# Both halves of the values as one stationary operand, and two places that follow

## The chip, the cores and the metric

The kernel runs on one core of one Trainium2 chip. The metric is the device time of one execution in microseconds, lower is better.

## The reference

Two transformer layers over one sequence of 512 tokens and 1024 features, all in float32. What the change touches is shown here: the values' product of the first layer's attention, the gates beta and the inverse of the second layer's delta rule.

```python
# layer 1, attention of 16 heads of 64, in query blocks of 128 (scores use softplus and a reverse cumsum)
    a = jnp.exp(log_a).astype(v.dtype)
    outs.append(jnp.einsum('bhts,bshd->bthd', a, v[:, :end]))
# layer 2, chunks of 64 tokens, 8 heads
beta = jax.nn.sigmoid(beta_logit)                       # beta_logit, a_dt: 16 columns of x @ w_in
g = -jnp.exp(a_log) * jax.nn.softplus(a_dt + dt_bias)
lower = jnp.where(strict, jnp.einsum('bhncd,bhnmd->bhncm', k_beta, k) * decay, 0.0)
t_inv = lax.linalg.triangular_solve(lower, eye, left_side=True, lower=True, unit_diagonal=True)
```

Around them stand the usual parts: norms, projections, a gated feed-forward part in layer 1, a second mixer (retention) and a squared-ReLU feed-forward part in layer 2.

## The kernel before

Tokens come in NT = 4 tiles of 128 and features in KD = 8 tiles of 128. Nearly every product keeps float32's precision by two rounded numbers for each operand: the upper part h (the value rounded to the fast type F32R) and the lower part l (what is left). `split_w` does this for weights (ACT makes h, DVE makes l), `evac_pair` for results in PSUM. A product then takes three passes (`mm3`): h by h, h by l and l by h; the l by l pass is left out. Small products of plain float32 operands (the delta rule) are single calls that the trace shows as two records each.

The attention of layer 1 (`attention`) is written as a loop over 48 banks, three for each head: the bank holds the scores of some key blocks b against the queries, as `BANKS` says (blocks 3 and 2 with 256 columns each, block 1 with 384, block 0 with 512). For each bank `z_bank` makes the scores, ACT and DVE make the softplus, `sums_bank` adds the cumulative sums by matmuls and makes the weights a, again as h and l, and `av_bank` multiplies them by the values into one PSUM bank of the head ("pso"). `z_bank` runs LAG = 3 banks ahead of `sums_bank`, and `av_bank` one behind. When a head's third bank is through, its result is split into h and l (ACT, then DVE) into the head's half of a pair of slots, which the output projection reads.

Two heads lie side by side in a result of 128 partitions, so a stationary tile of values holds 64 columns of each of two heads (vH or vL), and only one half of the 128 rows of the result is read.

Between the banks `run` lets other work for TensorE go on, the fill: the generator `others` gives the projections of queries and keys of the pairs 1 to 7 (`qk`), those of the values of heads 8 to 15 (`values`), and, at the end, the part of the output projection that is already possible (`out_part`). Each bank may issue BESIDE = 2300 ns of fill, counted in the kernel's own estimate of TensorE's time. When the loop comes to the scores of a pair whose queries are not yet there (`ready_q`), it takes fill without ration until they are. DVE also sums the conditioning's products here (`mod_sums`, L500), two for each of 24 steps.

The order on each engine's queue is set by the tile framework's scheduler from the order in the program, the dependences and its cost estimates. SP's queue issues the loads of weights.

In layer 2 `first_proj` projects the 16 columns of beta and a_dt together with the first heads' queries and keys in two halves of 256 tokens (`halved`), and `gates_and_decays` makes beta and the decays from them. `delta_inverse` builds the inverse of a unit triangular matrix of 128 x 128 in each of 4 chunk pairs of a head, from inverses of 32 x 32 that DVE has solved: it merges twice, and holds the result and its transpose side by side (X, Y), with each merge a few products of 128 x 128, four at a time (`prods`). Two of these generators run turn by turn with the projections and with the scans (`delta_scan`), at distances given by their `yield` values in ns.

Of the kernel before, what the change touches and what calls it, by code (L numbers as in the profile page):

```python
# [10 lines left out]
F32R = mybir.dt.float32r  # L11
# [6 lines left out]
P = 128  # L18
# [52 lines left out]
class Net:  # L71
# [83 lines left out]
    def halved(self, units, xT, first=None):  # L155

        for t0 in (0, 256):
            t = slice(t0, t0 + 256)  # L160
            for i, (acc, h, l) in enumerate(units):
                nk = h.shape[1]
                for k in range(nk):
                    xh, xl = xT[k]
                    self.mm3(acc[:, t], h[:, k, :], l[:, k, :], xh[:, t], xl[:, t],
                             k == 0 and t0 == 0, k == nk - 1, chk=True)
# [451 lines left out]
    def attention(self):  # L618
# [6 lines left out]
        def ev_v(g0):  # L625
            def ev(tt, acc):
                for g in range(g0, g0 + acc.shape[-1] // 256):
                    if tt == 0:
                        v[g] = [self.pair(), self.pair()]
                    t = v[g][tt // 2]  # L630
                    c = slice(tt % 2 * 256, tt % 2 * 256 + 256)
                    self.evac_pair(t[:, 0, c], t[:, 1, c], acc[:, (g - g0) * 256:(g - g0 + 1) * 256])
            return ev
# [57 lines left out]

        def values(g):
            r = self.raw(wqkv, 0, KD, 2 * D + g * 256, 256)
            hl = {}
            for c in (0, 4):
                h, l = self.split_w(r[:, c:c + 4, :], [P, 4, 256])
                for i in range(4):
                    hl[c + i] = (h[:, i, :], l[:, i, :])
            yield
            for tt in range(NT):  # L700
                if tt % 2 == 0:
                    bank = self.ps("g")
                acc = bank[:, tt % 2 * 256:tt % 2 * 256 + 256]
                t = slice(tt * P, (tt + 1) * P)
                for k in range(KD):
                    self.mm3(acc, hT[k][0][:, t], hT[k][1][:, t], *hl[k], k == 0 and tt % 2 == 0, k == KD - 1, chk=True)
                    if k % 4 == 3 and k < KD - 1:
                        yield
                ev_v(g)(tt, acc)
                yield  # L710
# [145 lines left out]
    def av_bank(self, n):  # L856
# [8 lines left out]
        for b, t0, c0, w in self.BANKS[bi]:  # L865
            c = b % 2 * 256 + pr % 2 * P
            vH, vL = self.v[pr // 2][b // 2][:, 0, c:c + P], self.v[pr // 2][b // 2][:, 1, c:c + P]
# [76 lines left out]
    def gates_and_decays(self, acc, heads):  # L944
# [3 lines left out]
        sm = self.t2()  # L948
        nc.vector.tensor_copy(sm[:16, :], acc[:16, :])
        dtb = self.bcast_row(a["dt_bias_2"][0], A_H, "dtb")  # L950
# [4 lines left out]
        for n in range(NT):  # L955
            nc.tensor.transpose(pt[:, n * 16:(n + 1) * 16], sm[:16, n * P:(n + 1) * P], self.ident[:16, :16])
        pv = pt[:, :64].rearrange("p (n c) -> p n c", c=16)

# [84 lines left out]
    def first_proj(self, heads):  # L1043

        nc, w = self.nc, self.a["w_in_2"][0]
        r = self.t2([P, KD, 16])
        nc.sync.dma_start(r, w[:, O_BE:O_BE + 16].rearrange("(k p) c -> p k c", p=P))
        hl = self.t2([P, 2, KD, 16], F32R)
        h, l = hl[:, 0], hl[:, 1]
        self.evac_pair(h, l, r)  # L1050
# [150 lines left out]
    def delta_inverse(self, heads):  # L1201
# [3 lines left out]
        for h in heads:  # L1205
# [484 lines left out]
```

## Time and profile before

| | |
|---|---|
| median of three runs | 2096.71 us (2095.53 to 2097.28) |
| the profiled execution | 2098.39 us, of which its span 2096.6 us |
| granted TensorE clock, mean over the span | 0.997 |
| TensorE (PE) busy | 2056.1 us, 98% of the span |
| VectorE (DVE), ScalarE (ACT), GpSimd (POOL) busy | 54%, 40%, 6% |
| the attention's heads | from about 80 to 298 us |
| gates and first projection of layer 2 | about 703 to 745 us |
| inverses and scans | 887 to 980 us and 1126 to 1230 us |

In the profile a row names line, engine, operation, the tiles written and read (psa, psg and pso are banks of PSUM; "pso<-s,s" from 85 to 298 us is the product with the values), the shape, the count, and then busy time and the mean of one in ns. The columns of matmuls of 512 take 0.39 us each but start every 0.23 us, since they overlap; so a matmul's price is its spacing, not its duration. L135 is the line of `mm`, through which most matmuls go; L269 and L270 are the two halves of `evac_pair`.

### The profile page before, as it was taken

The page shows a single profiled execution, that of the slowest core. Times are in us where ns is not written, and L with a number is a line of the kernel's source. Part 1 is how long each engine was busy: PE and PEld are TensorE (multiplying, and loading weights), DVE is VectorE, ACT ScalarE, POOL GpSimd, SP SyncE. Part 2 cuts the span into 40 slices and gives each one's busy share as a digit, 9 for nine tenths or more (in the row PEclk, how much of TensorE's full clock was granted, in tenths as well). Part 3 has the DMA queues.
Part 4 walks back from the last instruction along what each step waited for, and adds up shares of the span by engine and source line. Part 5 has one row for each costly group of instructions (what it writes and reads, how often), then busy time and mean ns, then how long its engine had stood idle before and what let it go on. Part 6 is the DMA issues. An engine that isn't in the chain of part 4 may idle for free.

```text
span 2096.6 us, 25166 instructions
## 1 busy us (share of the span) xinstructions
PE 2056.1 (98%) x10019; PEld 1724.0 (82%) x10019; DVE 1132.4 (54%) x1835; ACT 838.1 (40%) x1348; POOL 115.8 (6%) x171
## 2 busy tenths in 40 slices
PE   6999999999999999999999999999999999999998
PEld 5788878888888888887888788888888889888886
DVE  6689878333322565866667545344444475423433
ACT  3787764223212364344533432333232344323421
POOL 2000000000000113000320000000000000000000
PEclk9999999999999999999999999999999999999999
DMA  8545545323233344321342343222222553323322
GB/s 266 166 123 151 160 125 177 101 96 115 90 131 101 102 128 133 102 66 41 129 136 73 101 146 121 96 81 86 81 86 81 183 178 121 101 87 125 100 91 81
DMA packets 169687, 244.00 MB, mean 116 GB/s; under 512 B 14097, under 2 KB 112491, under 8 KB 169569
## 3 DMA queue, kind: packets, MB, share of 16 engines
q1 hardware_dynamic: 166092, 234.76, 34.1%
q0 software_dynamic: 3232, 7.34, 1.5%
q8 instruction: 79, 1.29, 0.3%
q14 instruction: 40, 0.32, 0.0%
q10 hardware_dynamic: 244, 0.29, 0.0%
HBM read 218.69 MB, written 19.42 MB: 114 GB/s over the span
## 4 chain that ended last, share of the span: by engine, by line
PE 91%; DVE 4%; DMA 2%; ACT 1%; issue 1%; POOL 1%; POOLq 0%; DVEq 0%; ACTq 0%; SPq 0%
PE psg L135 42%; PE psa L135 37%; PE pso L135 10%; PE psa L139 1%; DMA raw<-sb_w_qkv 1%; DVE wl L126 1%; DVE s L270 1%; DMA s<-ada_w 1%; DMA cv<-ada_w 0%; PE pso L322 0%; DVE s L1370 0%; PE pso L1513 0%; DMA s<-x 0%; PE pso L575 0%; POOL sm L1365 0%
## 5 line engine op out<-in xcount | busy, mean ns | idle before, releaser
L135 PE MATMUL psg<-s,wh 128*128 128x512 f32 x2368 | 744.6, 395 | 1.9 <-DVE s L270 1.7
L126 DVE TENSOR_TENSOR wl<-raw,wh 128x1024 fp32r<-128x1024 f32 x306 | 373.7, 1222 | 461.3 <-ACT wh L122 262.0
L135 PEld LDWEIGHTS psg<-s,wh 128*128 128x128 f32 x2368 | 440.0, 188 | 89.7 <-issue 2.1
L135 PE MATMUL psa<-wh,s 128*128 128x512 f32 x1536 | 479.5, 391 | 0.0
L135 PE MATMUL psg<-s,wl 128*128 128x512 f32 x1184 | 462.4, 391 | 0.0
L122 ACT CAST wh<-raw 128x1024 fp32r<-128x1024 f32 x202 | 212.2, 1053 | 416.5 <-PE psg L135 157.0
L135 PEld LDWEIGHTS psa<-wh,s 128*128 128x128 f32 x1536 | 289.5, 189 | 60.2 <-ACT s L272 0.3
L135 PE MATMUL psa<-wl,s 128*128 128x512 f32 x768 | 299.5, 390 | 0.3 <-DVE wl L126 0.3
L135 PEld LDWEIGHTS psg<-s,wl 128*128 128x128 f32 x1184 | 222.3, 188 | 46.4
L135 PEld LDWEIGHTS psa<-wl,s 128*128 128x128 f32 x768 | 144.8, 188 | 30.4 <-DVE wl L126 0.6
L125 ACT CAST wh<-raw 128x1024 fp32r<-128x1024 f32 x104 | 109.0, 1050 | 138.2 <-PE psg L135 109.0
L135 PE MATMUL psa<-s,s 128*128 128x512 f32 (+3 forms) x712 | 161.1, 359 | 0.0
L135 PEld LDWEIGHTS psa<-s,s 128*128 128x128 f32 x712 | 123.3, 189 | 20.5 <-DVE s L1318 0.9
L135 PE MATMUL pso<-s,wh 128*128 128x512 f32 x448 | 137.9, 389 | 0.0
L135 PE MATMUL psg<-wh,s 128*128 128x512 f32 (+1 forms) x416 | 132.0, 379 | 0.0
L135 PEld LDWEIGHTS pso<-s,wh 128*128 128x128 f32 x448 | 84.1, 188 | 17.5
L135 PE MATMUL pso<-s,wl 128*128 128x512 f32 x224 | 87.1, 389 | 0.0
L135 PEld LDWEIGHTS psg<-wh,s 128*128 128x128 f32 x416 | 75.1, 189 | 11.5 <-DVE s L270 0.4
L269 ACT CAST s<-t 128x512 fp32r<-128x512 f32 (+1 forms) x94 | 54.5, 594 | 59.5 <-DVE t L1604 40.7
L135 PE MATMUL psa<-s,wh 128*128 128x256 f32 x384 | 72.9, 291 | 2.3 <-DVE s L270 1.5
L135 PE MATMUL psg<-wl,s 128*128 128x512 f32 (+1 forms) x208 | 74.9, 360 | 0.0
L270 DVE TENSOR_TENSOR s<-t,s 128x512 fp32r<-128x512 f32 (+1 forms) x94 | 59.7, 654 | 20.1 <-ACT s L269 19.9
(250 smaller groups left out, 2144.9 us busy)
## 6 DMA issues: line engine op xcount, KB each, us to landing
raw<-w_in SPq DMA_DIRECT2D x56, 1024.0 KB, 5.2
raw<-ffn_w_in SPq DMA_DIRECT2D x22, 1024.0 KB, 5.1
cv<-ada_w SPq DMA_DIRECT2D x64, 256.0 KB, 2.8
raw<-w_up SPq DMA_DIRECT2D x16, 1024.0 KB, 5.3
raw<-w_down SPq DMA_DIRECT2D x16, 1024.0 KB, 5.0
raw<-sb_w_qkv SPq DMA_DIRECT2D x10, 1024.0 KB, 7.7
raw<-ffn_w_out SPq DMA_DIRECT2D x10, 1024.0 KB, 6.3
s<-ada_w SPq DMA_DIRECT2D x32, 256.0 KB, 6.6
```

What stands on the lines that cost most here:

```text
L122: nc.scalar.copy(h, src)
L125: nc.scalar.copy(h, src)
L126: nc.vector.tensor_sub(l, src, h.bitcast(F32))
L135: self.last_mm = self.nc.tensor.matmul(acc, lhsT, rhs, **kw)
L139: self.last_mm = self.nc.tensor.transpose(out, x, ident)
L269: nc.scalar.copy(dst_h, src)
L270: nc.vector.tensor_sub(dst_l, src, dst_h.bitcast(F32))
```

## The change

Values: the tiles now hold, for each head, its 64 columns of h beside its 64 columns of l. That tile is stationary, and two passes (the weights' h and l) give h's result in one half of the partitions and l's in the other, for one head. The two halves are added at the end of the head: ACT copies one half to a temporary tile in the head's own half, DVE adds the other half from PSUM, and the sum is split as before. So a head's last step is ACT, DVE, ACT, DVE where it was ACT, DVE. The l by l pass comes with it.

The values of heads 8 to 15 are projected in one go, 512 columns wide, after pair 3's queries, and no longer in two goes of 256 columns after pairs 3 and 5.

Gates: h and l of the 16 columns stand side by side as 32 stationary columns, in two passes; their rows are added after the transpose to tokens (one copy and one addition on DVE more).

Inverse: the transposed result Y1 of the first merge was a product of its own (four matmuls) and is now a transpose of X1 by TensorE, with a copy instead of an addition on DVE. It is made one step later, beside the next product.

```diff
# halved
+                    if l is None:
+                        for x in (xh, xl):
+                            self.mm(acc[:, t], h[:, k, :], x[:, t], start=k == 0 and t0 == 0 and x is xh,
+                                    stop=k == nk - 1 and x is xl, skip_group_check=True)
# attention, ev_v
-                    t = v[g][tt // 2]
-                    c = slice(tt % 2 * 256, tt % 2 * 256 + 256)
-                    self.evac_pair(t[:, 0, c], t[:, 1, c], acc[:, (g - g0) * 256:(g - g0 + 1) * 256])
+                    t = v[g][tt // 2][:, tt % 2, :].rearrange("p (h i d) -> p h i d", h=4, i=2)
+                    x = acc[:, (g - g0) * 256:(g - g0 + 1) * 256].rearrange("p (h d) -> p h d", h=4)
+                    self.evac_pair(t[:, :, 0, :], t[:, :, 1, :], x)
# attention, values and others
-        def values(g):
-            r = self.raw(wqkv, 0, KD, 2 * D + g * 256, 256)
+        def values():
+            for k0 in (0, 4):
+                r = self.raw(wqkv, k0, 4, 2 * D + S, S)
...
-                    self.mm3(acc, hT[k][0][:, t], hT[k][1][:, t], *hl[k], k == 0 and tt % 2 == 0, k == KD - 1, chk=True)
-                    if k % 4 == 3 and k < KD - 1:
+                    self.mm3(acc, hT[k][0][:, t], hT[k][1][:, t], *hl[k], k == 0, k == KD - 1)
+                    if k % 2 == 1 and k < KD - 1:
...
-                if pr in (3, 5):
-                    yield from values((pr + 1) // 2)
+                if pr == 3:
+                    yield from values()
# av_bank
-            mm(out[:, t], vH, ab[:, 0, cc], start=(b == 3), stop=False, skip_group_check=True)
-            mm(out[:, t], vH, ab[:, 1, cc], start=False, stop=False, skip_group_check=True)
-            mm(out[:, t], vL, ab[:, 0, cc], start=False, stop=(b == 0), skip_group_check=True)
+            v = self.v[pr // 2][b // 2][:, b % 2, h % 4 * P:h % 4 * P + P]
+            mm(out[:, t], v, ab[:, 0, cc], start=(b == 3), stop=False, skip_group_check=True)
+            mm(out[:, t], v, ab[:, 1, cc], start=False, stop=(b == 0), skip_group_check=True)
...
-        r = slice(e * 64, e * 64 + 64)
-        self.evac_pair(o[r, 0, :], o[r, 1, :], out[r, :])
+        r, r2 = (slice(i * 64, i * 64 + 64) for i in (e, 1 - e))
+        u = self.t2()
+        self.nc.scalar.copy(u[r, :], out[r2, :])
+        self.nc.vector.tensor_add(u[r, :], u[r, :], out[r, :])
+        self.evac_pair(o[r, 0, :], o[r, 1, :], u[r, :])
# gates_and_decays, first_proj
+        pv = self.const("pv", [P, NT, 16])
+        p2 = pt[:, :128].rearrange("p (n i c) -> p n i c", i=2, c=16)
+        nc.vector.tensor_copy(pv, p2[:, :, 0, :])
+        nc.vector.tensor_add(pv, pv, p2[:, :, 1, :])
...
-        self.qk_proj(0, [(acc[:16, :], h, l)], lambda: self.beside(self.gates_and_decays(acc, heads)))
+        self.qk_proj(0, [(acc[:32, :], hl.rearrange("p k i c -> p k (i c)"), None)], lambda: self.beside(self.gates_and_decays(acc, heads)))
# delta_inverse
-            nc.vector.tensor_add(Y1, Y0, prods(Pm, Y0))
...
-            yield 1200
+            pt = self.ps("a")
+            for n in range(NT):
+                cs = slice(n * P, (n + 1) * P)
+                self.tr(pt[:, cs], X1[:, cs], self.ident)
+            nc.vector.tensor_copy(Y1, pt)
+            yield 1500
```

How it moves instructions is seen at three places. A row gives the line, the operation, the tile written, the tiles read, and the shape; "x3" is three such rows in a run.

First TensorE at the end of the attention's steady fill. "psg" is the output projection's first part, "pso" the product with the values, "psa ... tri" the cumulative sums, "psa<-s,s" the scores. Before, the last steady fill stands ahead of head 13's third bank (bank 41 of 0 to 47):

```order
L135 MATMUL psg_2766<-wl_2758,s_118_2472 128x512
L135 MATMUL psg_2766<-wh_2757,s_118_2472 128x512
L135 MATMUL psa_2801<-s_47_522,tri 128x256 x6
L135 MATMUL pso_2842<-s_133_2878,s_104_2035 128x512 x3
L135 MATMUL psa_2928<-s_129_2724,s_124_2606 128x256 x2
```

After, it stands ahead of head 12's third bank (bank 38):

```order
L135 MATMUL psg_2559<-wl_2551,s_121_2421 128x512
L135 MATMUL psg_2559<-wh_2550,s_121_2421 128x512
L135 MATMUL psa_2586<-s_48_523,tri 128x256 x6
L135 MATMUL pso_2630<-s_129_2661,s_81_1311 128x512 x2
L135 MATMUL psa_2716<-s_125_2514,s_120_2393 128x256 x2
```

Behind both stand six more matmuls of the fill, between later banks; the loop's last banks without steady fill are the six from 42 in the one and the nine from 39 in the other.

Second DVE at the end of a head (head 0), the split of "pso" and what stands around it, before:

```order
L825 TENSOR_TENSOR cr_826<-t_820,cr_825 128x512
L854 TENSOR_TENSOR s_50_525<-t_846,s_50_525 128x384
L270 TENSOR_TENSOR s_61_835<-psg_749,s_61_835 64x512
L270 TENSOR_TENSOR s_62_866<-pso_773,s_62_866 64x512
L815 SCALAR_TENSOR_TENSOR t_877<-psa_869,t_877 128x384
```

After (L830, L859, L275 and L820 are the same lines, L888 is the new addition):

```order
L830 TENSOR_TENSOR cr_823<-t_817,cr_822 128x512
L859 TENSOR_TENSOR s_50_525<-t_843,s_50_525 128x384
L275 TENSOR_TENSOR s_61_832<-psg_749,s_61_832 64x512
L888 TENSOR_TENSOR t_863<-t_863,pso_773 64x512
L820 SCALAR_TENSOR_TENSOR t_876<-psa_868,t_876 128x384
L858 CAST s_63_897<-t_895 128x384
L505 SCALAR_TENSOR_TENSOR s_67_938<-cv_1126,csilu,s_67_938 128x512
L275 TENSOR_TENSOR s_62_862<-t_863,s_62_862 64x512
```

The bank of PSUM is now read by the addition at the place of the old split, and the split follows three rows later.

Third TensorE in the second pair of inverses. Before, each head's first merge takes the product of Y0 and Pm (t_7689 is the first head's Pm, t_7702 the other's) and then that of Pm and Y0:

```order
L135 MATMUL psa_7703<-s_251_7640,s_252_7647 128x128 x4
L135 MATMUL psa_7711<-t_7689,s_249_7608 128x128 x4
L135 MATMUL psa_7717<-s_249_7608,t_7689 128x128 x4
L135 MATMUL psa_7723<-s_238_7170,s_242_7433 128x256
L135 MATMUL psa_7728<-t_7702,s_251_7640 128x128 x4
L135 MATMUL psa_7734<-s_251_7640,t_7702 128x128 x4
L135 MATMUL psa_7740<-s_238_7170,s_225_6453 128x256
L135 MATMUL psa_7744<-t_7709,s_250_7615 128x128 x4
```

After, the second of them is gone and a transpose of X1 (t_7584) stands behind the product that follows:

```order
L135 MATMUL psa_7578<-s_251_7499,s_252_7506 128x128 x4
L135 MATMUL psa_7586<-t_7564,s_249_7483 128x128 x4
L135 MATMUL psa_7592<-s_238_7045,s_242_7308 128x256
L135 MATMUL psa_7597<-t_7577,s_251_7499 128x128 x4
L135 MATMUL psg_7633<-wh_7615,s_204_5556 128x512
L135 MATMUL psg_7633<-wl_7616,s_204_5556 128x512
L135 MATMUL psg_7633<-wh_7615,s_208_5560 128x512
L135 MATMUL psa_7637<-s_238_7045,s_225_6328 128x256
L135 MATMUL psa_7641<-t_7584,s_250_7490 128x128 x4
L139 MATMUL psa_7647<-cst,t_7584 128x128 x4
```

The products that follow have moved up, and three matmuls of a projection stand between the two steps.

More of the change, by code (lines that the diff above doesn't have):

```diff
@@ L164, in halved @@
                     xh, xl = xT[k]
-                    self.mm3(acc[:, t], h[:, k, :], l[:, k, :], xh[:, t], xl[:, t],
-                             k == 0 and t0 == 0, k == nk - 1, chk=True)
+                    if l is None:
+                        for x in (xh, xl):
+                            self.mm(acc[:, t], h[:, k, :], x[:, t], start=k == 0 and t0 == 0 and x is xh,
+                                    stop=k == nk - 1 and x is xl, skip_group_check=True)
+                    else:
+                        self.mm3(acc[:, t], h[:, k, :], l[:, k, :], xh[:, t], xl[:, t],
+                                 k == 0 and t0 == 0, k == nk - 1, chk=True)
                     self.poll()
@@ L690, in qk @@
             yield
-        def values(g):
-            r = self.raw(wqkv, 0, KD, 2 * D + g * 256, 256)
+        def values():
             hl = {}
[L695 to L699, printed above, removed]
+            for k0 in (0, 4):
+                r = self.raw(wqkv, k0, 4, 2 * D + S, S)
+                for c in (0, 2):
+                    h, l = self.split_w(r[:, c:c + 2, :], [P, 2, S])
+                    for i in range(2):
+                        hl[k0 + c + i] = (h[:, i, :], l[:, i, :])
+                    yield
             for tt in range(NT):
-                if tt % 2 == 0:
-                    bank = self.ps("g")
-                acc = bank[:, tt % 2 * 256:tt % 2 * 256 + 256]
+                acc = self.ps("g")
                 t = slice(tt * P, (tt + 1) * P)
                 for k in range(KD):
-                    self.mm3(acc, hT[k][0][:, t], hT[k][1][:, t], *hl[k], k == 0 and tt % 2 == 0, k == KD - 1, chk=True)
-                    if k % 4 == 3 and k < KD - 1:
+                    self.mm3(acc, hT[k][0][:, t], hT[k][1][:, t], *hl[k], k == 0, k == KD - 1)
+                    if k % 2 == 1 and k < KD - 1:
                         yield
-                ev_v(g)(tt, acc)
+                ev_v(2)(tt, acc)
                 yield
@@ L865, in av_bank @@
         for b, t0, c0, w in self.BANKS[bi]:
-            c = b % 2 * 256 + pr % 2 * P
-            vH, vL = self.v[pr // 2][b // 2][:, 0, c:c + P], self.v[pr // 2][b // 2][:, 1, c:c + P]
+            v = self.v[pr // 2][b // 2][:, b % 2, h % 4 * P:h % 4 * P + P]
             cc = slice(c0, c0 + w)
             t = slice(t0, t0 + w)
-            mm(out[:, t], vH, ab[:, 0, cc], start=(b == 3), stop=False, skip_group_check=True)
-            mm(out[:, t], vH, ab[:, 1, cc], start=False, stop=False, skip_group_check=True)
-            mm(out[:, t], vL, ab[:, 0, cc], start=False, stop=(b == 0), skip_group_check=True)
+            mm(out[:, t], v, ab[:, 0, cc], start=(b == 3), stop=False, skip_group_check=True)
+            mm(out[:, t], v, ab[:, 1, cc], start=False, stop=(b == 0), skip_group_check=True)
         if bi > 0:
@@ L948, in gates_and_decays @@
         sm = self.t2()
-        nc.vector.tensor_copy(sm[:16, :], acc[:16, :])
+        nc.vector.tensor_copy(sm[:32, :], acc[:32, :])
         dtb = self.bcast_row(a["dt_bias_2"][0], A_H, "dtb")
@@ L955, in gates_and_decays @@
         for n in range(NT):
-            nc.tensor.transpose(pt[:, n * 16:(n + 1) * 16], sm[:16, n * P:(n + 1) * P], self.ident[:16, :16])
-        pv = pt[:, :64].rearrange("p (n c) -> p n c", c=16)
+            nc.tensor.transpose(pt[:, n * 32:(n + 1) * 32], sm[:32, n * P:(n + 1) * P], self.ident[:32, :32])
+        pv = self.const("pv", [P, NT, 16])
+        p2 = pt[:, :128].rearrange("p (n i c) -> p n i c", i=2, c=16)
+        nc.vector.tensor_copy(pv, p2[:, :, 0, :])
+        nc.vector.tensor_add(pv, pv, p2[:, :, 1, :])
         def c3(name):
@@ L1047, in first_proj @@
         nc.sync.dma_start(r, w[:, O_BE:O_BE + 16].rearrange("(k p) c -> p k c", p=P))
-        hl = self.t2([P, 2, KD, 16], F32R)
-        h, l = hl[:, 0], hl[:, 1]
-        self.evac_pair(h, l, r)
+        hl = self.t2([P, KD, 2, 16], F32R)
+        self.evac_pair(hl[:, :, 0, :], hl[:, :, 1, :], r)
         acc = self.ps("g")
-        self.qk_proj(0, [(acc[:16, :], h, l)], lambda: self.beside(self.gates_and_decays(acc, heads)))
+        self.qk_proj(0, [(acc[:32, :], hl.rearrange("p k i c -> p k (i c)"), None)], lambda: self.beside(self.gates_and_decays(acc, heads)))
     def qk_proj(self, h, turn=(), first=None):
```

## The prediction

> **What bounds the kernel now.** I read the page's busy table and the chain that ended last first, then the waits of PE, then the busy time by stretches of the attention, then the order in time around each of the three places that change.
>
> ```profile
> span 2096.6 us, 25166 instructions
> PE 2056.1 (98%) x10019; PEld 1724.0 (82%) x10019; DVE 1132.4 (54%) x1835; ACT 838.1 (40%) x1348; POOL 115.8 (6%) x171
> PE 91%; DVE 4%; DMA 2%; ACT 1%; issue 1%; POOL 1%; POOLq 0%; DVEq 0%; ACTq 0%; SPq 0%
> ```
>
> PE is the bound nearly everywhere, so a matmul taken away is worth its spacing, unless another engine is close behind. In the attention one is (stretches from the table by windows: start and end, length, then busy time of PE, PEld, DVE, ACT and POOL, granted clock, DMA share):
>
> ```profile
> 100.00:125.00 25.00, 25.00 (x139) 21.14 (x138) 24.18 (x42) 21.03 (x40) 1.02 (x2) 1.00 0.68 201
> 125.00:150.00 25.00, 25.00 (x177) 23.10 (x176) 19.10 (x35) 19.24 (x37) 1.02 (x2) 1.00 0.26 74
> 150.00:175.00 25.00, 25.00 (x144) 21.25 (x144) 22.26 (x38) 20.56 (x37) 0.95 (x1) 1.00 0.43 137
> 175.00:200.00 25.00, 25.00 (x146) 21.49 (x145) 24.76 (x43) 20.22 (x36) 1.29 (x3) 1.00 0.59 168
> 200.00:225.00 25.00, 24.92 (x176) 22.45 (x175) 18.22 (x33) 19.88 (x39) 1.72 (x3) 1.00 0.32 99
> 225.00:250.00 25.00, 25.00 (x137) 21.23 (x136) 22.87 (x38) 15.07 (x28) 1.02 (x2) 1.00 0.57 174
> 250.00:275.00 25.00, 24.50 (x133) 20.01 (x133) 22.88 (x41) 21.68 (x43) 1.08 (x2) 1.00 0.66 191
> 281.00:297.00 16.00, 14.28 (x81) 11.27 (x80) 13.13 (x25) 13.85 (x26) 0.00 (x0) 1.00 0.20 67
> ...
> PE pso L516 <- ACT t L269: 1.0, 1, 1.0
> PE psa L135 <- DVE t L815: 0.6, 1, 0.6
> PE pso L135 <- DVE s L853: 0.5, 1, 0.5
> ```
>
> The last three rows are all the waits of PE from 100 to 298 us: 2.1 us. So PE is the bound there too, but DVE is busy 154.3 of 175 us (88%), and 24.8 of 25 where projections of queries and keys are the fill. The two slack windows (19.10 and 18.22) are those in which the fill is the values' projection. From 281 us the fill is used up, PE idles 1.7 of 16 us and ACT is the busiest of the others.
>
> **The change part by part.** First the spacing of matmuls, from the chain (start, us, count) and the time order:
>
> ```profile
> 101.50 0.68 PE pso L135 x3
> 110.33 0.54 PE pso L135 x3
> 149.62 1.44 PE psg L135 x12
> 367.88 5.44 PE pso L135 x24
> 155.53 0.84 PE L135 MATMUL pso<-s,s 128*128 128x512 f32 x3
> 239.41 0.84 PE L135 MATMUL pso<-s,s 128*128 128x512 f32 x3
> 280.89 0.85 PE L135 MATMUL pso<-s,s 128*128 128x512 f32 x3
> 289.07 0.39 PE L135 MATMUL pso<-s,s 128*128 128x512 f32 x1
> 296.78 0.73 PE L135 MATMUL pso<-s,s 128*128 128x512 f32 x2
> ```
>
> These give 0.18 us for a pass of 384 columns, 0.12 for 256 (the values' own) and 0.227 for 512; the rows of 512 columns are each a head's last product with the values (head 0's at 101.50), which clock the heads: 195.3 us from head 0's to head 15's at 296.78.
>
> Values of the attention: a head loses one pass of 256, 256, 384 and 512 columns, 0.12 + 0.12 + 0.18 + 0.23 = 0.65 us, 10.4 us for 16 heads. The values' projection for heads 8 to 15 goes from 192 passes of 256 (23.0 us) to 96 of 512 (21.8 us): 1.2 us. Together PE loses 11.6 us of work. Three things take from it.
>
> *Fill runs out earlier.* Fill is rationed at 2300 ns for each bank, a number that the change leaves alone. All of the values now come before pair 4's keys and queries, which the loop needs at bank 21. Up to there the fill is seven projections of 24 passes (5.44 us each) and the values' 21.8, 59.9 us, where 24 banks have granted 55.2; the rest is forced in at once and later banks have less. In the order of the changed kernel the steady fill ends three banks sooner (nine instead of six at the end). Without fill a head takes 8.2 and 7.7 us (280.89, 289.07, 296.78), 2.65 us a bank, where with it a head takes 14.0 (155.53 to 239.41, six heads). PE's own work in a bank, by columns and the spacing above, falls from 2.05 to 1.83 us. ACT's new copy lengthens such a bank by a third of 0.58. So PE idles 9 x (2.84 - 1.83) = 9.1 instead of 6 x (2.65 - 2.05) = 3.6 us: 5.5 of the 11.6 are lost.
>
> *DVE comes level.* The nearest rows to the new copy and addition:
>
> ```profile
> L270 DVE TENSOR_TENSOR s<-pso,s 64x512 fp32r<-64x512 f32 x15 | 10.3, 686 | 1.0 <-ACT s L269 0.8
> L269 ACT CAST s<-pso 64x512 fp32r<-64x512 f32 x16 | 9.3, 580 | 2.8 <-PE pso L135 2.5
> L913 DVE TENSOR_TENSOR t<-t,pso 128x512 f32<-128x512 f32 x20 | 13.8, 688 | 66.3 <-PE pso L135 66.3
> ```
>
> Half the partitions cost as much as all (686 beside 688), so 0.69 us on DVE and 0.58 on ACT for each head. From head 0's end to 281 us DVE has some 158 us of work at 88%; it gains 14 x 0.69 = 9.7 and hands three banks (some 3 us each, with the sums of the modulation) to the part behind the fill: 159 us. PE alone would take 196 - 6.1 - 25.6 = 164.3 us for that stretch (some 196 us before for the whole, 6.1 saved so far, 9 x 2.84 without fill), so DVE would have to be busy 97% of it. I take 2 us of waiting, between nothing (24.76 of 25 was reached with PE dense) and 16 us (DVE no busier than the 88% of before). The split of the values into strided halves has no row; I keep the 0.42 us of the 128x256 split, and twice that would add 2 us to DVE there. SP sends the same two transfers of 1 MB for it, now in a row, and the values hold all four split-weight buffers; I cost both at nothing, since the last token tile's 5.4 us of fill, spread over two banks, cover the next split, and without that cover the next projection would start one split (1 to 2 us) late.
>
> *The last head.* Its chain grows by a copy and an addition in series, 1.27 us. Nothing comes after it but the output projection, of which the changed order puts some ten matmuls ahead; I take 0.6.
>
> So the attention gains 11.6 - 5.5 - 2.0 - 0.6 = 3.5 us.
>
> The inverse, from the time order:
>
> ```profile
> 889.70 1.05 PE L135 MATMUL psa<-t,s 128*128 128x128 f32 x8
> 890.59 1.06 PE L135 MATMUL psa<-s,t 128*128 128x128 f32 x8
> 891.48 0.60 PE L139 MATMUL psa<-cst,cv 128*128 128x128 f32 x4
> 891.92 1.06 PE L135 MATMUL psa<-t,s 128*128 128x128 f32 x8
> ```
>
> Four products take 0.89 us (889.70 to 890.59) and four transposes 0.44. Replacing one by the other saves 0.45 us for each of 8 heads, 3.6 us. DVE's addition from PSUM becomes a copy from PSUM, so nothing is added there. The next product now follows the addition that makes X1 without the second product between; the other head's step covers that as the order stands. What it frees is lost where the scans wait next. I take 2.7 (1 to 3.6).
>
> The gates, and the clock:
>
> ```profile
> 700.00:712.00 12.00, 9.68 (x46) 8.34 (x45) 10.46 (x15) 7.27 (x15) 3.66 (x5) 0.75 0.31 87
> 707.31 0.63 PE L135 MATMUL psa<-s,wh 128*128 128x256 f32 x2
> 707.74 0.41 PE L135 MATMUL psa<-s,wl 128*128 128x256 f32 x1
> 713.55 2.68 PE L135 MATMUL psg<-s,t 128*16 128x256 f32 x22
> 716.07 1.03 PE L322 MATMUL pso<-cst,s 128*128 128x128 f32 x8
> 345.00:350.00 5.00, 3.10 (x27) 2.93 (x26) 5.00 (x9) 1.19 (x4) 0.00 (x0) 1.00 0.35 114
> ```
>
> 22 passes in 2.52 us are 0.115 each; 16 of 48 fall away: 1.8 us. The added copy and addition on 64 numbers are below 0.2 us each, behind dense matmuls. I take 1.5 (0 to 1.8). Just ahead of it PE had stalled and then ran at half pace (0.43 us for two passes of 256 at 707.31, 0.75 granted), which shifts of some us may deepen or cure. [...] But from 345 to 350 us PE idled 38% and the granted clock stayed 1.00, so the sum leaves it out.
>
> Sum: 3.5 + 2.7 + 1.5 = 7.7 us. The profiled execution took 2098.4 (its span plus 1.8), so 2090.7 in its terms; the median of the runs is 1.7 below it, 2096.7, so I predict 2089.0.
>
> **Rivals.**
> 1. Everything lands: the 11.6, 3.6 and 1.8 us, 17.0 in all: 2079.7. The 99% window speaks for it; the three extra banks without fill, which are in the order, speak against.
> 2. DVE holds PE, no net change: at a DVE share of 91% the stretch takes 159 / 0.91 = 174.7 us instead of 166.3, 8.4 worse than the sum has it: 2097.4. For it: two engines at 97% seldom run free of each other, and products with the values wait on DVE's subtraction just behind ACT's exponent. Against: only 1.1 us of PE's waits were on DVE.
> 3. DVE decides, slower: if it gets no busier than the 88% of before, 159 / 0.88 + 25.6 = 206.3 us instead of 196, less 4.2 from the other two parts: 2102.8. The kernel is slower by 0.2% from a share under 88.9%, and faster by 0.2% from one above 93.3%.
> 4. The clock: at half pace, as at 707 us, PE's 16.5 us in nine banks become 33.0 where 25.6 are there, and some 6 us of the output projection take 3 more: 10.4 worse, 2099.4. The row at 345 us speaks against. [...]
>
> **How the numbers follow.** My forecast (2085 to 2092.5) has 0.54; rival 1 has 0.14, rival 2 has 0.20, rival 3 has 0.08, rival 4 has 0.04. 0.2% of 2096.7 is 4.2 us, about what a measurement of this kernel can tell from no change. The forecast and rival 1 are faster: 0.68; rivals 2 and 4 within: 0.24; rival 3 slower: 0.08. The range, 2080.5 to 2098.5, leaves out part of rivals 1 and 4 and all of 3.
>
> **What would show it.** Right: the spans of heads with fill fall from 14.0 to about 13.2 us, DVE shows 24 or more of 25 us in nearly every stretch up to the end of the fill, about nine banks at 2.8 us stand behind it, PE's waits on DVE in the attention grow from 1 to some 3 us, and the scan stage shortens by 2 to 4 us. Wrong: PE's waits on DVE of 8 us or more (rival 3), a granted clock under 1 at the attention's end (rival 4), or a new order that opens or closes a stall elsewhere, above all near 700 us, where 2 to 3 us hang on the clock.

## The result and the profile after

| | before | after |
|---|---|---|
| median | 2096.71 us | 2086.53 us (2084.46 to 2086.63, five runs) |
| ratio of the times | | 0.995, 95% interval 0.9938 to 0.9962 |
| profiled execution | 2098.39 us, span 2096.6 | 2084.46 us, span 2082.7 |

The change makes the kernel about 10 us faster (10.2 between the medians), 0.5%; 2089.0 us had been forecast. First the page of the changed kernel: span, busy time of each engine, the chain that ended last.

```profile
span 2082.7 us, 24796 instructions
PE 2039.8 (98%) x9811; PEld 1703.4 (82%) x9811; DVE 1141.2 (55%) x1853; ACT 848.7 (41%) x1368; POOL 115.7 (6%) x171
PE 88%; DVE 4%; issue 3%; DMA 2%; ACT 1%; POOL 1%; DVEq 0%; POOLq 0%; ACTq 0%
```

PE lost 16.3 us of busy time and 208 matmuls, and the span 13.9 us. Now the attention in the stretches shown of before (start and end, length, busy time of PE, PEld, DVE, ACT and POOL, granted clock, DMA share, GB/s), then all filled heads, from head 0's last product to head 12's.

```profile
100.00:125.00 25.00, 25.00 (x138) 21.08 (x137) 24.48 (x42) 21.56 (x41) 1.02 (x2) 1.00 0.49 153
125.00:150.00 25.00, 25.00 (x138) 21.15 (x138) 21.46 (x39) 20.21 (x40) 2.02 (x3) 1.00 0.53 147
150.00:175.00 25.00, 25.00 (x135) 20.73 (x134) 23.88 (x43) 21.70 (x43) 0.00 (x0) 1.00 0.28 88
175.00:200.00 25.00, 23.27 (x118) 19.07 (x117) 22.57 (x36) 14.81 (x28) 1.02 (x2) 1.00 0.66 189
200.00:225.00 25.00, 24.97 (x137) 20.64 (x135) 22.15 (x39) 23.53 (x44) 1.02 (x2) 1.00 0.46 127
225.00:250.00 25.00, 24.89 (x133) 20.77 (x134) 24.07 (x43) 21.71 (x40) 1.98 (x3) 1.00 0.45 127
250.00:275.00 25.00, 24.51 (x142) 20.02 (x141) 23.60 (x44) 20.73 (x42) 1.08 (x2) 1.00 0.60 189
281.00:297.00 16.00, 13.44 (x56) 9.16 (x56) 14.20 (x24) 12.68 (x23) 0.00 (x0) 1.00 0.29 105
98.90:264.50 165.60, 163.73 (x879) 136.68 (x878) 153.27 (x261) 136.17 (x255) 8.13 (x14) 1.00 0.50 146
```

DVE reaches 24 us in two of the seven stretches only; over the filled heads it is busy 153.27 of 165.60 us, 93%. Where PE idles is new: 1.7 us between 175 and 200 us, where ACT falls to 14.81. The waits of PE from 100 to 298 us name it (in all, count, longest):

```profile
PE pso L135 <- DVE s L859: 2.3, 3, 1.8
PE psa L135 <- DMA s<-s: 1.7, 1, 1.7
PE psa L135 <- ACT t L856: 0.6, 1, 0.6
```

The time order of PE (start, duration, row, idle time ahead and what ended it) gives the place, head 8's first scores:

```profile
192.27 0.47 PE L135 MATMUL psa<-s,s 128*128 128x256 f32 x2 [1.73 <-DMA s<-s]
```

"s<-s" is the copy by which the queries of a pair reach the other half of the partitions (L692, issued on POOL). The projection of pair 4's queries now has the values ahead of it, so it is forced in at once and is finished just before its use. The largest wait on DVE, 1.8 us, is in the last head, behind the fill.

Where the 13.9 us came from is read from the starts of the same matmuls in two traces. The table gives, for each stretch of the first trace of before (us from its start), by how many us it became longer (+) or shorter (-); 601 to 690 us is the same in all. The other kernels in it are experiments, told below.

| | to 88 us | 88-335 attention | 335-601 | 690-769 gates | 769-1003 | 1003-1245 | rest |
|---|---|---|---|---|---|---|---|
| before, second trace | -2.3 | +0.1 | +1.5 | -0.1 | 0.0 | 0.0 | +0.4 |
| inverse alone | -1.8 | -0.3 | +1.5 | -1.9 | -2.2 | -1.8 | +0.4 |
| gates alone | -2.4 | -0.1 | 0.0 | -4.1 | 0.0 | -0.1 | +0.5 |
| attention alone | -2.1 | -4.0 | -0.1 | -1.4 | 0.0 | 0.0 | +0.9 |
| the change | -2.2 | -3.7 | -0.1 | -3.6 | -2.2 | -1.8 | -0.2 |
| values split | -1.2 | -3.8 | -0.2 | -4.1 | -2.0 | -1.9 | +0.3 |

### The profile page after: what moved, and what is told of

Its sections match the earlier page's. It is cut to its first block, busy times and chain, and to the rows that moved or that the text cites. A ratio compares the mean times of both kernels' runs of the same rounds, so it can differ in the third digit from the quotient of the medians.

```text
span 2082.7 us, 24796 instructions
## 1 busy us (share of the span) xinstructions
PE 2039.8 (98%) x9811; PEld 1703.4 (82%) x9811; DVE 1141.2 (55%) x1853; ACT 848.7 (41%) x1368; POOL 115.7 (6%) x171
## 4 chain that ended last, share of the span: by engine, by line
PE 88%; DVE 4%; issue 3%; DMA 2%; ACT 1%; POOL 1%; DVEq 0%; POOLq 0%; ACTq 0%
PE psg L135 41%; PE psa L135 37%; PE pso L135 9%; PE psa L139 1%; DMA s<-ada_w 1%; DVE s L275 0%; PE pso L327 0%; DVE s L1386 0%; DVE wl L126 0%; DMA cv<-ada_w 0%; PE pso L1529 0%; DMA s<-x 0%; DVE s L301 0%; PE pso L580 0%; DVE s L505 0%
## 5 line engine op out<-in xcount | busy, mean ns | idle before, releaser
L126 DVE TENSOR_TENSOR wl<-raw,wh 128x1024 fp32r<-128x1024 f32 x306 | 373.5, 1222 | 454.9 <-ACT wh L122 257.8
L135 PEld LDWEIGHTS psa<-s,s 128*128 128x128 f32 x712 | 123.2, 189 | 24.5 <-issue 2.0
L135 PE MATMUL psg<-wh,s 128*128 128x512 f32 x352 | 129.0, 416 | 0.0
L274 ACT CAST s<-t 128x512 fp32r<-128x512 f32 (+2 forms) x110 | 64.3, 596 | 63.4 <-DVE t L1620 40.7
L275 DVE TENSOR_TENSOR s<-t,s 128x512 fp32r<-128x512 f32 (+2 forms) x110 | 70.6, 658 | 21.6 <-ACT s L274 21.1
L135 PEld LDWEIGHTS psg<-wh,s 128*128 128x128 f32 x352 | 66.2, 188 | 13.3 <-ACT s L274 0.2
L135 PE MATMUL psg<-wl,s 128*128 128x512 f32 x176 | 69.6, 396 | 0.0
```

Of the source, the lines that this page charges most:

```text
L126: nc.vector.tensor_sub(l, src, h.bitcast(F32))
L135: self.last_mm = self.nc.tensor.matmul(acc, lhsT, rhs, **kw)
L274: nc.scalar.copy(dst_h, src)
L275: nc.vector.tensor_sub(dst_l, src, dst_h.bitcast(F32))
```

## Experiments: each part alone, and before once more

**The inverse alone** (edit: the hunk of `delta_inverse`, nothing else).

> The kernel before with the change of the inverse alone (Y1 as the transpose of X1). Theory A, the matmul engine's work counts in full: 8 heads x 0.45 us = 3.6 us, so 2093.1 us, and in the trace both stretches with inverses (887 to 985 and 1126 to 1230 us of before) end about 2 us earlier each, as they did in the whole change (2.2 and 1.8). Rival B, the prediction's term: the scans' waits take a quarter back, 2.7 us, 2094.0 us, some 1.3 us a stretch. Rival C, the gain there came from the other parts (a new phase of the scans): 1 us or less, 2095.7 us or more. Ahead of 880 us nothing should differ by more than the clock near 700 us moves it.

Measured: 2092.56 us, ratio 0.9981 (0.9972 to 0.9990). Both stretches with inverses are shorter as in the whole change, 2.2 and 1.8 us, and they are unchanged in every kernel without this part. So the 3.6 us of work land in full, and the first stretch gains some 0.4 us more (over all kernels with this part, below too, the two stretches gain 3.6 to 4.2 us). Theory A holds; the quarter that the prediction let the scans take back is not taken. The order of PE there in the changed kernel:

```profile
880.06 1.05 PE L135 MATMUL psa<-t,s 128*128 128x128 f32 x8
880.95 0.60 PE L139 MATMUL psa<-cst,cv 128*128 128x128 f32 x4
881.39 1.06 PE L135 MATMUL psa<-t,s 128*128 128x128 f32 x8
```

The second product (0.89 us) of before is gone between the first two rows, and nothing waits there.

**The gates alone** (edit: the hunks of `halved`, `gates_and_decays` and `first_proj`).

> The kernel before with the change of the gates alone (32 stationary columns, two passes). Theory A: 16 passes x 0.115 us = 1.8 us, 2094.9 us, and the stretch at half pace near 707 us stays 5 to 6 us long as before. Rival B: all of the 3.5 us that the whole change gained between 690 and 760 us belong to this part, 2093.2 us, because the order around the gates changes and with it the length of the half pace (2.3 us in the whole change, 5.9 before). Rival C: the copy and addition in its chain take it back, 2096.7 us.

Measured: 2094.72 us, ratio 0.9987 (0.9978 to 0.9996). The stretch from 690 to 769 us shrank by 4.1 us, but the kernels without the gates' change gained there too, from 0.1 to 1.9 us. The stretches with the granted clock (the figure ahead of the last two) tell why. First before's second trace:

```profile
705.00:710.00 5.00, 4.41 (x21) 3.97 (x21) 4.55 (x9) 1.33 (x3) 2.57 (x3) 0.50 0.09 12
```

The changed kernel, whose stall lies 6 us earlier:

```profile
700.00:705.00 5.00, 4.30 (x26) 4.33 (x27) 4.56 (x10) 2.01 (x6) 2.56 (x3) 0.66 0.14 26
```

And the gates alone:

```profile
705.00:710.00 5.00, 4.87 (x43) 4.59 (x42) 4.55 (x9) 2.51 (x6) 1.81 (x3) 1.00 0.43 125
```

At half pace the passes behind that stall came late by some 2.6 us in both traces of before (in the second, 27 passes from 705.89 to 711.82 us, 0.22 us apart, where 0.12 is the full pace), by 1.4 with the inverse alone, by 1.3 with the attention alone and after the change, and not at all with the gates alone. Late passes were not all lost time where a wait for DVE followed them: with the inverse alone such a wait of 0.7 us is gone (PE's waits from 690 to 760 us are 1.6 us in all, 2.3 in before), so 0.7 of its 1.4 us were lost, and the 1.9 us that it gained there are the clock's: 2.6 - 0.7. The kernels told below as another ration, the DVE copy with a tile of its own and the split with more lead have the changed gates and no half pace there, and they gain 4.1 us like the gates alone; the change gained 3.6, so its half pace cost 0.5. Less the clock, the gates are worth 4.1 - 2.6 = 1.5 us, alone and in the others, near theory A's 1.8. The expectation that the half pace would stay at 5 to 6 us in length was a miss: it is not the kernel's own.

**The attention alone** (edit: the hunks of `ev_v`, `values`, `others` and `av_bank`).

> The kernel before with the change of the attention alone (values as halves side by side, values of heads 8 to 15 in one go). Theory A: from head 0's start to 330 us it gains 3.8 us as in the whole change, where the rest of that profile's 6.1 us at 350 us was the clock's start-up and a late weight transfer ahead of the heads, which no edit touches: 2092.9 us. Rival B: the 6.1 us are all the change's: 2090.6 us, and the two steps ahead of 80 us (0.8 and 1.0 us) appear here again. In both, heads 1 to 5 last 12.8 us (13.5 before), head 7's span holds a wait of 1.5 to 2 us for a transfer of the queries' copies, and nine banks without fill take 2.7 us each.

Measured: 2092.68 us, ratio 0.9977 (0.9968 to 0.9987). Heads 1 to 4 last 12.8 us, the attention gains 4.0 us, and the 2.1 us ahead of it are those that the kernels with an unchanged attention show too. Theory A. Head 8's wait for the copy was 0.9 us here instead of 1.5 to 2.

**Before once more**, for a second trace.

> The kernel before once more, for a second trace of it. Theory A (some 3.5 us of the 13.9 between the two profiled executions are chance): the first projection for the heads starts 1 to 2 us earlier than the 80.1 us of the first trace, the stretch at half pace near 707 us has another length than 5.9 us, the heads and both stretches of inverses agree with the first trace within 0.3 us, and the span is 2093 to 2096 us. Rival B (the first trace is typical): all four agree with the first trace within 0.3 us, 2096.6 us.

Measured: span 2096.0 us. The heads start 2.3 us earlier, so that much of the 13.9 us is the first trace's late start, and heads and inverses repeat within 0.1 us. Of what the start gave, a new stretch at half pace took 1.5 us back, at a place where the first trace had a granted clock of 1.00:

```profile
345.00:350.00 5.00, 4.61 (x27) 4.64 (x28) 4.86 (x11) 1.45 (x4) 0.00 (x0) 0.66 0.46 124
```

Theory A holds but for two points: the start moved by more than its 1 to 2 us, and the half pace near 707 us cost the same as in the first trace.

Without chance, then: attention 3.7 to 4.0, gates 1.5, inverse 4.0 to 4.1, 9.2 to 9.6 us. The three parts alone gave 0.19, 0.13 and 0.23%, 11.5 us, where the whole gave 10.5 by its ratio; the intervals cover the difference.

## Experiments: what the attention lost

11.6 us of passes went and 3.8 us were gained. The stretch from the same fill ahead of head 0 to the same matmul of the output projection, before:

```profile
80.10:332.20 252.10, 248.75 (x1415) 211.07 (x1416) 210.41 (x358) 188.02 (x351) 13.40 (x23) 1.00 0.47 142
```

And after:

```profile
77.90:326.20 248.30, 240.77 (x1254) 196.37 (x1255) 219.87 (x374) 194.25 (x368) 13.37 (x22) 1.00 0.47 140
```

161 matmuls fewer, 8.0 us less busy time (a pass behind a wait counts with its whole duration, 0.50 us for the one of 512 columns at 288.98 us instead of the spacing of 0.227; by my estimate that is why it is not 11.6), and 4.2 us more idle time: 7.5 for 3.4. It sits in three places: the filled heads (1.9 us in heads 1 to 12, where heads 1 to 13 of before have 0.6), the banks without fill (3.7 for 1.7), and the part behind the last head's last product (1.9 for 1.0). This last part, up to the same matmul of the output projection, before:

```profile
297.20:332.20 35.00, 34.00 (x157) 27.43 (x156) 24.40 (x39) 16.42 (x35) 3.14 (x6) 1.00 0.50 163
```

And after:

```profile
289.10:326.20 37.10, 35.15 (x157) 27.51 (x158) 26.27 (x41) 18.77 (x39) 3.10 (x5) 1.00 0.38 122
```

So 2.1 us are lost there with as many matmuls. It is no chance: the part takes 35.1 us in all four traces with the old product with the values, and 36.9 to 37.2 in all five with the new one and no half pace there. Nearly half has a row, two waits for an addition of the next norm on DVE (before, PE waited 1.0 us at these tiles):

```profile
PE pso L327 <- DVE s L303: 1.9, 2, 1.1
```

Two passes of the modulation that stood ahead of the last product are 0.5 us more, and the rest has no single row.

**The values split again.**

```diff
# values(g) as before the change: 256 columns in each of two goes
...
-                if pr == 3:
-                    yield from values()
+                if pr in (3, 5):
+                    yield from values((pr + 1) // 2)
```

> The changed kernel with the values of heads 8 to 15 projected in two goes of 256 columns again, after pairs 3 and 5, instead of one of 512 after pair 3. Theory F (what the change loses, it loses by the order of the fill): 1.2 us more matmul work, but head 7 loses its wait of 1.7 us, the fill reaches four or five banks further, which saves 4 to 5 x 0.9 us: 3 to 5 us faster than the changed kernel, 2081.5 to 2083.5 us. Rival P (matmul work alone counts): 1.2 us slower, 2087.7 us. Rival D (DVE holds the filled heads): the banks that become filled run at DVE's pace and nothing is gained, 2086.5 us, with waits of the matmul engine on DVE of 3 us or more between 200 and 275 us.

Measured: 2085.59 us, ratio 0.9944 (0.9932 to 0.9957); the attention gained 3.8 us, as the whole change did. Theory F was too good: head 7's wait is gone and the fill reaches further, but now pair 6's queries are forced in at once (head 11 lasts 17.7 us, 13.4 being the mean of heads 1 to 12, with a wait of 1.3 us on DVE), and the output projection ran at half pace, where the changed kernel's trace shows 1.00:

```profile
290.00:295.00 5.00, 5.00 (x16) 3.93 (x16) 4.46 (x6) 3.31 (x5) 0.00 (x0) 0.66 0.14 23
```

That is the prediction's rival 4, in another kernel: 9 passes that take 3.65 us where the changed kernel takes 2.09, so 1.6 us.

**Another ration.** Heads 1 to 7 get more fill, later ones less:

```diff
+            ns = 700 if self.proj else 1800 if self.ready_q >= 4 else 2700
...
-            self.run(fill, self.BESIDE // 2)
+            self.run(fill, ns // 2)
...
-                self.run(fill, self.BESIDE - self.BESIDE // 2)
+                self.run(fill, ns - ns // 2)
```

> The changed kernel with another ration of the fill: 2700 ns a bank until pair 4's queries are projected, 1800 from there until the output projection is the fill, 700 in it, where the changed kernel has 2300 throughout. The work is the same; no projection is forced in at once any more, and steady fill lasts to bank 41 instead of 38. Theory F (the order of the fill costs what the changed kernel lost): head 7's wait of 1.7 us goes and three more banks have fill, 3 x 0.9 us: 4.4 us faster than the changed kernel, 2082 us. Rival D (DVE and the matmul engine are level in the filled heads): DVE's share in 100 to 250 us rises from 92% to 95% or more, waits on DVE there grow to 3 us or more, and at most 1 us is gained, 2085.5 us or more. Rival C (the clock): as with the values split, the granted clock falls at the attention's end and takes back some 1.7 us, 2083.8 us.

Measured: 2093.21 us, ratio 0.9985 (0.9976 to 0.9993), 6.7 us slower than the changed kernel: none of the three. DVE was not in the way (131.7 of 150 us busy from 100 to 250 us, where the changed kernel has 138.6). The ration was too exact: pairs 4 and 5 were now both finished just before their use, and PE stood 2.6 us ahead of head 8 and 2.7 us ahead of head 10, here the second:

```profile
217.56 0.47 PE L135 MATMUL psa<-s,s 128*128 128x256 f32 x2 [2.70 <-DMA s<-s]
```

Behind each of the two waits PE ran 3.4 us at half pace (from 191.4 and 218.7 us), and once more from 297.2 us. These waits and the passes that came late at half pace (some 1.5 us in each stretch) are, less the changed kernel's own wait of 1.7 us, about what the attention lost against it: 8 us. That gave theory L: a pair has to be finished well ahead.

**More lead, values in one go** (the same edit with 3000, 1900 and 700).

> The changed kernel with a ration of 3000 ns a bank until pair 4's queries are projected, 1900 from there, 700 in the output projection. Unlike 2700 and 1800, this finishes each pair's queries some two banks ahead of their first use. Theory L (what costs is a pair of queries that is finished just before its use, since the copy between partitions takes 3 to 6 us to land): no wait of the matmul engine on a transfer is left in the attention; the 1.7 us and some 1 us of the restart behind it are gained: 2083.5 to 2084.5 us. Rival W (a front-loaded fill costs as much as it gains: unfilled banks come earlier): 2086.5 us within 1. Rival D (DVE holds the pace as soon as fill per bank falls): 2089 us or more with waits on DVE above 3 us.

Measured: 2097.08 us, ratio 0.9997 (0.9988 to 1.0006). No scores wait for a copy any more, as theory L said, but the time is worse than with the wait: heads 3 and 4 last 19.5 and 15.5 us. SP issues a 1 MB load of the denser fill at 125.0 us and five rows of the modulation's weights behind it from 126.3 us; the sums over these rows (L505) stand in DVE's queue ahead of the attention's work, and DVE waits for the row:

```profile
134.46 0.75 DVE L505 SCALAR_TENSOR_TENSOR s<-cv,csilu,s 128x512 f32<-128x512 f32 x1 [4.18 <-DMA cv<-ada_w]
```

Stretches at half pace (from 140.8, 277.3 and 710.8 us) are in the loss too.

**More lead, values split** (the values in two goes, 2500 throughout, 700 in the output projection).

> The changed kernel with the values of heads 8 to 15 in two goes of 256 columns after pairs 3 and 5, a ration of 2500 ns a bank and 700 in the output projection. Theory L: 1.2 us more matmul work, but every pair's queries are finished ahead of use (no wait at heads 7 and 11, 2.5 us each way), and fill reaches bank 43 instead of 38 (5 x 0.9 us): 1.2 - 2.5 - 4.5 = 5.8 us faster than the changed kernel, 2080.7 us. Rival W (what the fill's order gains, the clock and the chain of the last heads take back, as in the first split): 2085 to 2086.5 us.

Measured: 2085.56 us, ratio 0.9942 (0.9930 to 0.9955). All waits of PE from 80 to 298 us that the profile lists:

```profile
PE pso L135 <- DVE s L859: 1.4, 1, 1.4
PE pso L135 <- DVE s L860: 1.0, 3, 0.4
PE psa L135 <- DVE s L831: 0.7, 2, 0.5
```

And the clock in the last head:

```profile
285.00:290.00 5.00, 4.55 (x10) 2.87 (x11) 3.98 (x7) 3.49 (x6) 0.00 (x0) 0.54 0.00 0
```

The waits went as theory L has it, and the attention still gained only 3.6 us: rival W. From 285.4 to 292.2 us the clock was at half. Two further runs put passes that nobody reads into the last head's waits.

```diff
+            if n >= 45:
+                w = self.ps("a")
+                for i in range(6):
+                    self.mm(w, self.v[3][1][:, 0, :P], self.v[3][1][:, 1, :], start=i == 0, stop=i == 5)
             if n >= 1:
                 self.av_bank(n - 1)
```

> The run before with the values split and every pair's queries ahead of use, with 24 further passes of 512 columns in the attention's last head, into PSUM banks that nobody reads, put where the matmul engine waits for the values' operand. In the run before, the clock was granted at half from 285.7 to 292.5 us, which cost 3.4 us. Theory K (idle stretches of the last heads bring the half pace on): the granted clock stays at 1.00 from 280 to 300 us, 3.4 us are gained and the passes cost at most 2 us of that, since most lie in waits: 2083 to 2084 us. Rival N (the half pace does not hang on these waits): it stays, and the passes cost 24 x 0.227 = 5.4 us less the 2.5 us of waits that they fill: 2088.5 us.

> The changed kernel with the same 24 passes in its last head, where its own trace shows no half pace. Theory K: nothing is gained in a run like that one; the passes cost what does not fit into the waits of 1.8, 0.2, 0.2 and 0.2 us there, 1 to 3 us: 2087.5 to 2089.5 us. If the changed kernel's other runs do fall to half pace there, which one trace cannot tell, the time is 2085 to 2086.5 us.

Measured: 2085.69 us, ratio 0.9949 (0.9937 to 0.9962), on the split with lead, and 2086.61 us, 0.9954 (0.9941 to 0.9968), on the changed kernel. The first one's clock stayed up:

```profile
285.00:290.00 5.00, 5.00 (x28) 4.40 (x27) 4.82 (x9) 4.07 (x6) 0.00 (x0) 1.00 0.01 3
```

Its attention gained 5.2 us, 1.6 more than without the passes and the most of all kernels, as theory K said of the trace; in the changed kernel, which had no half pace to cure, they cost 1.7 us (2.0 gained for 3.7). The medians show neither: both differ from those without the passes by 0.1 us, and the second lies between the two ranges that were expected. One trace each does not tell how often the half pace comes, so theory K is open, and no version is shown to beat the changed kernel by more than the intervals.

## Experiments: DVE

One more DVE copy at each head's end, 10.7 us of work that nobody waits for. First into a tile of its own:

```diff
         self.nc.vector.tensor_add(u[r, :], u[r, :], out[r, :])
+        self.nc.vector.tensor_copy(self.t2()[r, :], out[r, :])
```

> The changed kernel with one more DVE copy from PSUM of 64x512 at each head's end, into a tile that nobody reads: 16 x 0.67 us = 10.7 us of DVE work off every chain, as much again as the addition that the change put there. Theory A (DVE still has slack where the fill is, the matmul engine holds the pace): 0 to 2 us slower than the changed kernel, 2086.5 to 2088.5 us, the heads with fill stay at 12.8 us. Rival D (the prediction's DVE comes level, 159 us of work for 164): from 100 to 250 us DVE was busy 138.6 of 150 us, 7.4 us more make 97%, and the heads with fill grow by half a microsecond or more each: 2091 to 2096 us, with waits of the matmul engine on DVE of 4 us or more there.

Measured: 2097.04 us, ratio 1.0000 (0.9991 to 1.0009): the whole gain gone, 1 us past the range of rival D, but by another way, since heads 1 to 5 last 12.7, 13.3, 12.9, 12.8 and 15.2 us, nearly as in the changed kernel. The extra tile could be the reason, so the copy went next into the unread half of the addition's own tile:

```diff
+        self.nc.vector.tensor_copy(u[r2, :], out[r2, :])
```

> The changed kernel with one more DVE copy from PSUM of 64x512 at each head's end, as in the run before with a tile of its own, but now written to the half of the addition's own tile that nobody reads, so that it takes no buffer. Theory D (DVE's time is what counts: the wait for pair 4's queries grows with DVE's backlog, and the banks without fill are DVE's): 8 us or more slower than the changed kernel, 2095 us, the wait before head 8's first product again near 3.9 us, heads 1 to 4 still 12.8 to 13.3 us. Theory B (the extra tile of the earlier run did the harm): at most 3 us slower, 2086.5 to 2089.5 us, the wait near 1.7 us as in the changed kernel.

Measured: 2100.39 us, ratio 1.0015 (1.0006 to 1.0023). Theory D: the tile was not the reason. Heads 1 to 6 in the changed kernel:

```profile
98.90:176.90 78.00, 78.00 (x426) 65.60 (x425) 72.79 (x128) 66.17 (x127) 3.04 (x5) 1.00 0.44 131
```

With the copy:

```profile
100.90:178.80 77.90, 77.90 (x425) 65.60 (x424) 75.46 (x132) 65.95 (x126) 3.04 (x5) 1.00 0.40 115
```

DVE went from 93 to 97% and these heads took not a tenth of a microsecond more. The loss comes behind them, first in the wait ahead of head 8:

```profile
197.47 0.77 PE L135 MATMUL psa<-s,s 128*128 128x256 f32 x2 [5.04 <-DMA s<-s]
```

The way from DVE's lateness to PE leads through SP's queue. A raw tile of weights is free when DVE has made its lower part (L126), and a tile cv when DVE has added it up (L505, for which SP waited 94.3 us in the changed kernel from 80 to 290 us); SP issues the next transfer only then, in its order. SP's waits for L126 in the same stretch, changed kernel:

```profile
SPq L111 <- DVE wl L126: 31.9, 9, 7.1
```

With the copy:

```profile
SPq L111 <- DVE wl L126: 52.0, 10, 10.0
```

So the 1 MB transfer of the weights that is issued at 177.95 us in the changed kernel is issued at 185.84 us with the copy (2.0 us of it are the later start of its heads), and meets the two copies of pair 4's queries. The DMA issues around them (count, size of one, us from issue to landing), changed kernel:

```profile
s<-s POOLq DMA_DIRECT2D x2, 256.0 KB, 4.8
```

With the copy:

```profile
raw<-sb_w_qkv SPq DMA_DIRECT2D x1, 1024.0 KB, 7.7
s<-s POOLq DMA_DIRECT2D x2, 256.0 KB, 7.6
```

That the load makes the copies land later is argued from the order in time; no run shows it by itself. At head 9 every link is in the waits: 3.7 us were lost there, ACT waited 3.2 us for the output projection's weights, and PE 2.6 us for ACT. Of the rest, the two heads without fill 13 and 14 lost 3.6 us, and stretches at half pace are in these sums.

## Why the prediction was right, point by point

**Sum.** 7.7 us were forecast. Without chance the traces show 9.2 to 9.6, the medians 10.2: right in sign and cause, short by about 2 us. That the attention's part came out so near is luck in part, since its terms erred against each other.

**Work of the attention, 11.6 us.** Right: 161 matmuls fewer, and heads 1 to 4 fell by 0.7 us (12.8 for 13.5), the step's 0.65. Of "13.2 for 14.0" as what the trace would show, the mean was wrong: heads 1 to 12 took 165.6 us, 13.8 each, because head 7 takes 24.0 with its forced projections and twice the fill.

**Fill runs out earlier, 5.5 us lost.** Right in kind: from head 12's last product to head 15's are nine banks and 24.5 us,

```profile
264.30 0.63 PE L135 MATMUL pso<-s,s 128*128 128x512 f32 x2
...
288.98 0.50 PE L135 MATMUL pso<-s,s 128*128 128x512 f32 x1 [0.23 <-DVE s L859]
```

so 2.72 us a bank instead of 2.84. With the step's 1.83 us of work a bank 8.0 us stand idle, and before 3.4 (two heads in 15.7 us, six banks at 2.05): 4.6 us lost. A bank without fill grew by 0.1 us (2.62 before), where the step gave it a third of 0.58.

**DVE comes level, 2 us.** The size of the stretch was right (165.6 us, 166.3 forecast), the reason was not. DVE had 153.3 us of work there, not 159, and was busy 93%, not 97; no wait of PE on it in the filled heads is long enough to be listed. What was lost besides the tail and the end is 11.6 - 4.6 - 2.1 - 3.8 = 1.1 us, and it has a row: 1.7 us on the copy of pair 4's queries, where before PE waited 0.5 us (on DVE, L853) in its filled heads. The step saw that the queries were forced in at once, and costed it as fill alone, without the copy that follows. More DVE work did cost, but not through the share of busy time: the run with the in-place copy lost more than the copy's own time, 13.9 us between the medians for 10.7, by way of SP's queue and with stretches at half pace. Rivals 2 and 3 fall for the changed kernel, since their price was DVE's share of busy time, and 97% held nothing up in heads 1 to 6.

**The last head, 0.6 us.** Too small: 2.1 us were lost behind its last product (37.1 us for 35.0). The chain that the step had in mind, the head's own end, is not listed among PE's waits, since matmuls of the output projection run from 289.50 us on; the two waits that grew come later, at the norm behind the output projection. The step had looked no further than the head.

**Attention, 3.5 us.** Measured 3.7 to 4.0. Its terms erred against each other: 0.9 us too much lost at the tail and 0.9 in the filled heads, 1.5 too little behind the last product.

**The inverse, 2.7 us.** Mis-sized: 4.0 to 4.1 us, above its range of 1 to 3.6. The quarter that the scans would take back was an assumption without a row; the added transposes wait for nothing.

**The gates, 1.5 us.** Measured 1.5. The added copy and addition took 0.22 and 0.21 us, a little over the step's bound.

**The clock.** That 2 to 3 us hang on it near 700 us was right: 0 to 2.6 us among the traces, 2.1 of them in favour of the changed kernel, which the sum had not counted. Rival 4, half pace at the attention's end, did not come in the changed kernel's trace (1.00 from 281 to 297 us) but in six of the nine other kernels with the new product with the values, in one or two stretches each that begin between 277 and 304 us. So 0.04 was too low if it hangs on chance, and its price of 10.4 us too high: the values-split run lost 1.6 us by it.

**Rival 1**, everything lands, was 7 us off: the tail without fill alone excludes it.

## What to carry to other kernels

Cost a result that is forced in at once by all that follows it, its copies too, and look at how far ahead of its first use it stood before. A busy share of 97% on the second engine does not say that it holds the first (here heads 1 to 6 took 77.9 us with DVE at 97%, and 78.0 at 93%); ask instead which queue waits for its buffers to come free. Follow a cost to the first matmul from which both kernels are alike again: 2 us were lost here behind the last row that the step had looked at. And where a span of one trace moves more than the medians, compare the parts that the change doesn't touch before explaining it.

## What was not expected of the hardware

Half pace is no property of a place. The stall near 700 us is in all traces, and the passes behind it came late by 2.6, 2.6, 1.4, 1.3, 1.3 and 0 us in those of before, the parts alone and the change; near 348 us the same program ran once at 1.00 and once at 0.66. In the values-split run the longest single wait ahead of the half pace at 290 us was 1.8 us, and the changed kernel has the same wait in the same place at full clock. The stretches of half pace were 3.4 or 6.8 us long, apart from the one at the very end of each trace. At these two places no gap of PE ahead of them was longer than 1.8 and 0.84 us, while the share of idle time was high (PE busy 2.98 of 5 us ahead of 290 us, 3.36 of 5 near 700 us). What brings the half pace on is not shown. Two such stretches, the changed kernel's near 700 us and that of the first trace of before:

```profile
700.20:703.60 3.40, 2.90 (x14) 2.93 (x15) 2.96 (x8) 1.22 (x4) 2.56 (x3) 0.50 0.02 5
706.00:712.80 6.80, 6.12 (x29) 5.94 (x29) 5.81 (x11) 3.04 (x6) 3.02 (x4) 0.50 0.35 108
```

The longest gaps ahead of the half pace, in the values-split run:

```profile
287.66 0.84 PE L135 MATMUL pso<-s,s 128*128 128x384 f32 x2 [1.79 <-DVE s L859]
```

and near 700 us in the first trace of before:

```profile
704.70 0.39 PE L135 MATMUL psa<-s,wh 128*128 128x256 f32 x1 [0.84 <-DVE s L270]
```

The 256 KB copies of pair 4's queries between partitions landed in 4.8 us in the changed kernel and in 7.6 us beside a 1 MB load of weights from another queue; no run took the load alone away, and the changed kernel's other copies from 100 to 290 us took from 2.8 to 6.4 us, so the load is not shown to be the cause.
